# Block 1's mixer in another order: two RWKV chains among the projections, three output tiles open at once

## The chip, the cores and the metric

The kernel runs on one core of a Trainium2 chip. The metric is the device time of one execution in microseconds; a smaller time is better. The profile is of one execution on that core. Its engines are TensorE (PE; PEld is its weight load), VectorE (DVE), ScalarE (ACT), GpSimd (POOL) and SyncE (SP), which issues the transfers. Each engine takes its instructions strictly in the order of its own queue.

## What is computed

The reference runs three model blocks one after another on one sequence of 512 positions with 1024 channels, in float32. The change touches the mixer of the first block only:

```python
h = rmsnorm(x, norm_mix) * (1 + sc1) + sh1          # sc1, sh1, g1 ... from silu(c) @ w_mod + b_mod
p_fox, p_rwkv, p_moba = split(h @ w_in)
y_fox  = fox_attention(fq, fk, fv, ff)              # 4 heads of 64, causal softmax, forget gates added to the logits
y_rwkv = rwkv7_time_mix(p_rwkv, ...)                # 8 heads of 64, recurrence S_t = S diag(w) - (S kk)(kk a)^T + v k^T
y_moba = moba_attention(mq, mk, mv)                 # 4 heads of 64, blocks of 256: over 512 positions plain causal softmax
x = x + g1 * (concat(y_fox, y_rwkv, y_moba) @ w_out)
```

Behind it come the feed-forward part of block 1, a second block (attention, gating and convolution layers) and a third (state-space and convolution mixer).

## The kernel before

Activations lie with channels on the partitions, as tiles of 128 x 512. A float32 product is made of three products of the faster type: weights and activations are each split into a high part and a rest, and `mm3` (L298 to L300) issues high x high, high x rest and rest x high for each slice of 128 input channels. `wsplit` brings a weight tile: SP loads `wr` (two buffers), ACT casts it to `wh` (L277), DVE subtracts to `wl` (L279); `wh` and `wl` have three buffers each. `fm` makes one output tile of 128 channels in 24 matmuls of 512 columns, `tm` (L372 to L374) the two value projections with tokens on the partitions. PSUM has four tags, `mm`, `pa`, `pb` and `pt`, of two buffers each.

The mixer, `block1_mix`, consists of generators that issue work piece by piece:

- `keys` and `proj_rv` make the RWKV projections (keys; receptance and value) of four tiles, two heads each. `proj_rv` forms RO on POOL (L1017), the bonus on DVE (L1018) and sums it over a head on PE (L1023). After the fourth, `proj_r` makes the gate's projection `gl`.
- `proj_fox` and `proj_moba` make the values, then four query and key tiles each (`fqk`, tag `aq`).
- `blocks` (`rwkv_blocks`) prepares for each tile the inverse of a triangular matrix: a product on PE, the 16 x 16 diagonal blocks gathered over DRAM by SP, then 15 rounds of two small operations on DVE (L728, L729, here called the block chain), a cast to VT on ACT (L731, L732), a write to DRAM (L734) and a read back as T and TT (L737).
- `inverses` (`rwkv_inverse`) doubles the blocks to 128 x 128: products on PE (L752 is the first that needs T, L757, L760, and so on), copies on ACT, subtractions on DVE.
- `chain` (`rwkv_chain`) is the recurrence over four pieces of 128 positions, for one tile: transposes (L815), products among keys (L695, masked on DVE, L831, to `Ak`), L843 with `Ak`, then for each piece L853 to L872, which go from PE to ACT (L858) to PE to DVE (L854, L870, L872) and back; last the output (L879 to L882), a group norm (L887 to L896, its power on POOL, L895), a transpose (L900) and the gate (L906, L907).
- the two causal attentions (`attn`): two head pairs, per pair eight steps over 128, 256, 384 and 512 keys, for two heads each. A step's first half is logits on PE (L623, for fox L626, then L627 the mask) in `pt`, the maximum `nmx` on DVE (L565) and `P`, the exponential, on ACT (L568); its second half transposes `P` on PE (L577), copies it to `PT` on ACT (L580), multiplies by the values (L585) and scales on ACT (L590). The second half of a step is issued behind the first half of the next. A finished pair is transposed (L596), copied to `ya` (L618) and split (L286, L289). The four results are `yf0`, `yf1` (fox) and `ym0`, `ym1` (moba).
- `mods` makes the modulation vectors: a weight tile times a row and a sum over it on DVE, in one piece (L395) or in two halves (L386).

The order in which the pieces are issued is written by hand as two strings, one letter for one piece of a generator: `ORDER` (L2105) for the projections, with k keys, r receptance and value, f fox, m moba, b blocks, i inverses, a fox attention; then `REST` (L2103), with 0 to 3 for the four chains, i, a fox, m moba attention, d modulation. What they leave is woven (`weave`). A scheduler then places every instruction in its engine's queue by this priority and by the time at which it takes its inputs to be ready. Behind it, all output tiles are made from eight slices of input: `yf0`, `yf1`, the four chains' results, `ym0`, `ym1`.

In the kernel before the four chains run beside the fox and moba attention. Chains 0 and 1 use `pa` and `pb`, chains 2 and 3 both `mm`; the eight output tiles use `mm` one after another (the last two together).

## Time and profile before

| | us |
|---|---|
| median of 3 timed runs | 3099.59 |
| lowest and highest of them | 3094.19, 3102.67 |
| the profiled execution | 3092.06 |
| its span, first to last instruction | 3090.3 |
| mean granted TensorE clock over it | 0.975 of full |
| PE busy | 2911.2 (94%) |
| DVE busy | 2031.3 (66%) |
| ACT busy | 1164.4 (38%) |
| POOL busy | 679.0 (22%) |

The mixer of block 1 takes the first 512 us or so of the span: projections from some 30 us, the fox attention from 296 us, output tiles from 451 us. In a timeline a line gives start, length, engine, line, operation and tiles; "x4" are four in a row, and brackets tell how long the engine was idle before and what ended it. PEclk is the clock that TensorE was granted, as a share of 2.4 GHz; a 0.5 is 1.2 GHz. The matmuls are pipelined: their listed lengths overlap, and the time between two starts is what one costs.

### The profile page before, as it was taken

The numbers are of one execution on the slowest core, as the hardware profiler recorded it, in microseconds if no ns is written. First come the engines' busy times: TensorE is split into PE (matmuls) and PEld (weight loads), VectorE is DVE, ScalarE is ACT, GpSimd is POOL, SyncE is SP. The second block draws the span as 40 slices with busy tenths as digits, with TensorE's granted clock in tenths as the row PEclk, the third lists the DMA queues.
The fourth block names the chain that finished last, engine by engine and source line by source line (L and its number), as shares of the span: only waits on it lengthen the run. The fifth ranks groups of instructions, "written<-read, shape, count | busy, mean of one in ns | idle before, by whom it ended". The sixth has DMA issues, their size and how long they took to land. (4 is left out here: it accounts for less than half of the span.)

```text
span 3090.3 us, 40017 instructions
## 1 busy us (share of the span) xinstructions
PE 2911.2 (94%) x15254; PEld 2436.7 (79%) x15254; DVE 2031.3 (66%) x3398; ACT 1164.4 (38%) x1945; POOL 679.0 (22%) x582
## 2 busy tenths in 40 slices
PE   5999999999999988999999999999899998999998
PEld 3777878888877777888889788888788877877776
DVE  7766467665458577566564556364786978689764
ACT  4432433323333544332333333233444434442242
POOL 3222011000144253200001120001133333323312
PEclk9998999999999999999999999999999999999999
DMA  6334024463322123236343223333212222333332
GB/s 225 102 108 139 17 94 150 120 211 100 89 76 82 52 86 103 79 102 198 102 149 118 69 89 93 99 97 93 84 55 85 66 82 60 111 109 116 97 112 79
DMA packets 139681, 316.74 MB, mean 102 GB/s; under 512 B 25760, under 2 KB 51936, under 8 KB 139488
## 3 DMA queue, kind: packets, MB, share of 16 engines
q1 hardware_dynamic: 139488, 314.18, 32.9%
q8 instruction: 120, 1.97, 0.3%
q14 instruction: 73, 0.60, 0.1%
HBM read 298.92 MB, written 15.20 MB: 102 GB/s over the span
## 5 line engine op out<-in xcount | busy, mean ns | idle before, releaser
L279 DVE TENSOR_TENSOR wl<-wr,wh 128x1024 fp32r<-128x1024 f32 (+2 forms) x415 | 506.1, 1220 | 474.0 <-ACT wh L277 455.9
L277 ACT CAST wh<-wr 128x1024 fp32r<-128x1024 f32 (+2 forms) x457 | 455.7, 997 | 955.2 <-PE mm L299 461.3
L298 PE MATMUL mm<-hi,wh 128*128 128x512 f32 (+1 forms) x1844 | 711.3, 387 | 9.5 <-ACT csg L1396 4.2
L300 PE MATMUL mm<-hi,wl 128*128 128x512 f32 (+1 forms) x1844 | 708.0, 384 | 10.3 <-DVE wl L279 10.3
L299 PE MATMUL mm<-lo,wh 128*128 128x512 f32 (+1 forms) x1844 | 708.0, 385 | 2.2 <-DVE lo L289 1.2
L298 PEld LDWEIGHTS mm<-hi,wh 128*128 128x128 f32 x1844 | 351.6, 191 | 82.4 <-ACT csg L1396 5.5
L300 PEld LDWEIGHTS mm<-hi,wl 128*128 128x128 f32 x1844 | 352.5, 191 | 80.8 <-DVE wl L279 12.3
L299 PEld LDWEIGHTS mm<-lo,wh 128*128 128x128 f32 x1844 | 351.9, 191 | 71.5 <-DVE lo L289 2.7
L288 POOL CAST hi<-us 128x512 fp32r<-128x512 f32 x66 | 42.4, 643 | 873.6 <-DVE us L1196 855.3
L300 PE MATMUL pt<-hi,wl 128*128 128x512 f32 (+1 forms) x485 | 175.8, 363 | 4.0 <-DVE wl L279 4.0
L298 PE MATMUL pt<-hi,wh 128*128 128x512 f32 (+1 forms) x485 | 175.1, 361 | 0.0
L299 PE MATMUL pt<-lo,wh 128*128 128x512 f32 (+1 forms) x485 | 175.0, 361 | 0.0
L372 PE MATMUL mm<-wh,hi 128*128 128x256 f32 (+1 forms) x512 | 151.0, 295 | 18.8 <-DVE cv L1219 8.8
L298 PE MATMUL pb<-hi,wh 128*128 128x512 f32 (+1 forms) x445 | 165.2, 371 | 0.0
L299 PE MATMUL pb<-lo,wh 128*128 128x512 f32 (+1 forms) x445 | 165.0, 371 | 0.0
L300 PE MATMUL pb<-hi,wl 128*128 128x512 f32 (+1 forms) x445 | 164.9, 371 | 0.0
L300 PE MATMUL pa<-hi,wl 128*128 128x512 f32 (+1 forms) x420 | 161.3, 384 | 0.0
L298 PE MATMUL pa<-hi,wh 128*128 128x512 f32 (+1 forms) x420 | 160.9, 383 | 0.0
L299 PE MATMUL pa<-lo,wh 128*128 128x512 f32 (+1 forms) x420 | 160.8, 383 | 0.0
L1417 DVE SCALAR_TENSOR_TENSOR u<-csg,vec,u 128x400 f32<-128x400 f32 (+9 forms) x208 | 157.7, 768 | 3.7
L373 PE MATMUL mm<-wl,hi 128*128 128x256 f32 (+1 forms) x512 | 148.2, 290 | 0.8 <-DVE wl L279 0.6
L456 POOL TENSOR_TENSOR acc<-acc,sq 128x512 f32<-128x512 f32 (+1 forms) x63 | 86.7, 1385 | 281.2 <-ACT sq L451 230.8
(757 smaller groups left out, 5613.9 us busy)
## 6 DMA issues: line engine op xcount, KB each, us to landing
wr<-f_up SPq DMA_DIRECT2D x88, 512.0 KB, 3.5
wm<-w_mod SPq DMA_DIRECT2D x152, 256.0 KB, 5.0
wr<-w3x SPq DMA_DIRECT2D x56, 512.0 KB, 3.6
wr<-w_up SPq DMA_DIRECT2D x44, 512.0 KB, 3.6
wr<-w3c SPq DMA_DIRECT2D x40, 512.0 KB, 3.6
wr<-f_down SPq DMA_DIRECT2D x32, 512.0 KB, 3.5
wr<-w SPq DMA_DIRECT2D x29, 512.0 KB, 3.6
wr<-w_down SPq DMA_DIRECT2D x16, 512.0 KB, 3.6
```

The lines of the kernel that those rows point to most:

```text
L277: nc.scalar.copy(h, r)
L279: self.lo_engs[self.nlo % len(self.lo_engs)].tensor_tensor(l, r, h.bitcast(FT), OP.subtract)
L288: getattr(nc, hi_eng).tensor_copy(h, x)
L298: nc.tensor.matmul(ps, a, xh, start=first and i == 0, stop=False)
L299: nc.tensor.matmul(ps, a, xl, start=False, stop=False)
L300: nc.tensor.matmul(ps, b, xh, start=False, stop=last and i == n - 1)
L372: nc.tensor.matmul(ps, xh, a, start=k == 0, stop=False)
L373: nc.tensor.matmul(ps, xh, b, start=False, stop=False)
L456: (eng or nc.gpsimd).tensor_tensor(acc[:, hs], acc[:, hs], s, OP.add)
L1417: nc.vector.scalar_tensor_tensor(r8(o)[:, :, a:b], src, w(k), r8(o)[:, :, a:b], OP.mult, OP.add)
```

## The change

The chains get buffer tags of their own. `rwkv_chain` takes three more arguments: the tag of what lives through the chain (the transposed tiles and the state S), the tag of short-lived tiles, and that of the second set of products. Chains 0 and 1 now have PSUM tag `pt` and take their tiles from `aq` (chain 1 also from `g`), where the queries and keys lie; chains 2 and 3 have `pa` and `pb`.

The chains are created before the loop over `ORDER`, and 0 and 1 are issued inside it: chain 0 from behind the third group of inverse pieces, chain 1 behind it. The gate's projection, which a chain's end needs, becomes a generator of its own (g) and comes early. The fox values come later, the queries and keys of both attentions last, those of moba beside the first fox steps. `REST` has chains 2 and 3 beside the fox attention and the moba attention behind it, with the modulation pieces (d) spread. The first six output tiles go to `mm`, `pa`, `mm`, `pb`, `mm`, `pa`, so that three can be open at once, filled with the slices that are ready while the moba attention runs.

```diff
-    def rwkv_chain(self, i, K, gl, out, tag):
+    def rwkv_chain(self, i, K, gl, out, tag, kept, short, short2):
...
-            tok[nme] = self.t2(nm="tok" + nme, tag="h")
+            tok[nme] = self.t2(nm="tok" + nme, tag=kept)
...
-        def inner(lhs, rhs, strict, scale=None, tag="i"):
+        def inner(lhs, rhs, strict, scale=None, tag=short):
...
-        RV = self.t2(nm="RV", tag="i")
+        RV = self.t2(nm="RV", tag=short)
...
-        S = self.t2(nm="S", tag="h")
+        S = self.t2(nm="S", tag=kept)
...
-        A = list(zip(inner(kt, RO, 0), inner(bt, RO, 0, d2, "g")))
+        A = list(zip(inner(kt, RO, 0), inner(bt, RO, 0, d2, short2)))
...
-        wa, gl = self.t2(nm="wa"), self.accs[1]
+        wa, gl = self.t2(nm="wa"), [self.accs[1]]
...
-            yield from self.rwkv_chain(i, P[i], gl, yr[i], tag)
+            yield from self.rwkv_chain(i, P[i], gl[0], yr[i], *tag)
...
-            self.mix_evac(self.fm(A["w1"][1], xs), 1, gl)
-            self.sigmoid(gl, gl)
+
+        def proj_g():
+            self.mix_evac(self.fm(A["w1"][1], xs), 1, gl[0])
+            self.sigmoid(gl[0], gl[0])
             yield
...
-        gens = dict(k=keys(range(4)), f=proj_fox(), m=proj_moba(), r=proj_r(), i=inv, a=None, d=md, b=blocks())
+        ch = [chain(i, CTAG[i]) for i in range(4)]
+        gens = dict(k=keys(range(4)), f=proj_fox(), m=proj_moba(), r=proj_r(), g=proj_g(), i=inv, a=None, d=md, b=blocks())
+        gens.update(zip("0123", ch))
...
-        for c in "kbfmr":
+        for c in "kbfmrg":
...
-        ch = [chain(i, CTAG[i]) for i in range(4)]
...
-            done(i, self.fm(A["w_out"][i], ys))
+            done(i, self.fm(A["w_out"][i], ys, WOT[i]))
...
-CTAG = ("pa", "pb", "mm", "mm")
+CTAG = (("pt", "aq", "aq", "aq"), ("pt", "aq", "g", "g"), ("pa", "h", "i", "g"), ("pb", "h", "i", "g"))
+WOT = ("mm", "pa", "mm", "pb", "mm", "pa")
...
-REST = "aaiiidaiaiaiaiaiaaaaaaaaaaaaaaaaaaaaaaa0aaaa21ammmmdd0m1323mmmdd0123mmmmdd0123mm2mmdd013mmdmimd0121d3m2mmd03mmmmdd0123mdmmmdd012m3mmmdd"
+REST = "2a3a2a3ad2a3aad2aa3aad2aa3aad2aa3aad2aa3aad2aa3aadamamammmmdmmmdmmmdmmmdmmmdmmmd"
...
-ORDER = "krkrbbkfiiirribbkfriiirbfibfmfbiiiibrraiimmmamaiaaaaa"
+ORDER = "krkrbbkiiirribb0k0gr0iii0r0bi0b0r001f1iii1bi1r1b1f1f1f1fiiifmimamamamaaaa"
```

In the new code the lines of the mixer stand one to four further down (L728 is unchanged, L1018 becomes L1019, L1146 becomes L1150). Three places show what the new strings do to the queues; each tile's number tells instances apart.

The first is DVE's queue in the block chain of inverse 0, from its step of 48 elements a row. Before:

```order
L688 RECIPROCAL d_147_739<-d_147_739 128x8
L728 TENSOR_TENSOR btmp_628<-UV_624 64x48
L1045 TENSOR_TENSOR fz_742<-mm_783,fb 128x4
L729 TENSOR_TENSOR UV_624<-UV_624,btmp_628 64x4x12
L728 TENSOR_TENSOR btmp_628<-UV_624 64x55
L729 TENSOR_TENSOR UV_624<-UV_624,btmp_628 64x5x11
L728 TENSOR_TENSOR btmp_628<-UV_624 64x60
L729 TENSOR_TENSOR UV_624<-UV_624,btmp_628 64x6x10
L728 TENSOR_TENSOR btmp_628<-UV_624 64x63
L729 TENSOR_TENSOR UV_624<-UV_624,btmp_628 64x7x9
```

and now:

```order
L728 TENSOR_TENSOR btmp_628<-UV_624 64x48
L279 TENSOR_TENSOR wl_1174<-wr_1172,wh_1173 128x1024
L729 TENSOR_TENSOR UV_624<-UV_624,btmp_628 64x4x12
L635 SCALAR_TENSOR_TENSOR rM_866<-mm_867,vec_94,rM_866 128x511
L728 TENSOR_TENSOR btmp_628<-UV_624 64x55
L1019 SCALAR_TENSOR_TENSOR kp_536<-rM_866,vec_94,kp_536 128x512
L729 TENSOR_TENSOR UV_624<-UV_624,btmp_628 64x5x11
L728 TENSOR_TENSOR btmp_628<-UV_624 64x60
L729 TENSOR_TENSOR UV_624<-UV_624,btmp_628 64x6x10
L728 TENSOR_TENSOR btmp_628<-UV_624 64x63
```

Between the steps L728 and L729 there stood only the sum L1045 for the fox forget gates; now a weight split (L279), the evacuation of a receptance tile (L635) and the bonus (L1019) stand there. The product that waits for the bonus (tile kp_536) is the bones matmul on PE.

The second is DVE's queue at the first steps of the fox attention, with nmx (L565) and the modulation tiles (L395). Before:

```order
L780 TENSOR_SCALAR TT_2072<-pb_2398 64x4x64
L395 SCALAR_TENSOR_TENSOR wm_3202,modr<-wm_3202,act 128x1024
L395 SCALAR_TENSOR_TENSOR wm_3319,modr<-wm_3319,act 128x1024
L1127 TENSOR_TENSOR mod<-modr,vec_94 128x8
L395 SCALAR_TENSOR_TENSOR wm_3397,modr<-wm_3397,act 128x1024
L635 SCALAR_TENSOR_TENSOR acc_87<-mm_2409,vec_94,acc_87 128x511
L565 TENSOR_REDUCE nmx_2448<-pt_2444 128x1
L565 TENSOR_REDUCE nmx_2459<-pt_2455 128x1
L789 TENSOR_TENSOR X_2466<-X_2466,pa_2468 128x512
L570 RECIPROCAL rinv_2453<-sm_2451 128x1
L395 SCALAR_TENSOR_TENSOR wm_3418,modr<-wm_3418,act 128x1024
```

and now:

```order
L565 TENSOR_REDUCE nmx_2777<-pt_2773 128x1
L570 RECIPROCAL rinv_2782<-sm_2780 128x1
L395 SCALAR_TENSOR_TENSOR wm_3030,modr<-wm_3030,act 128x1024
L395 SCALAR_TENSOR_TENSOR wm_3088,modr<-wm_3088,act 128x1024
L395 SCALAR_TENSOR_TENSOR wm_3242,modr<-wm_3242,act 128x1024
L395 SCALAR_TENSOR_TENSOR wm_3299,modr<-wm_3299,act 128x1024
L395 SCALAR_TENSOR_TENSOR wm_3512,modr<-wm_3512,act 128x1024
L565 TENSOR_REDUCE nmx_2862<-pt_2858 128x1
L395 SCALAR_TENSOR_TENSOR wm_3539,modr<-wm_3539,act 128x1024
L570 RECIPROCAL rinv_2867<-sm_2865 128x1
L279 TENSOR_TENSOR wl_3928<-wr_3926,wh_3927 128x1024
L565 TENSOR_REDUCE nmx_2880<-pt_2876 128x1
```

Before, all but one of the twelve L395 stood ahead of the first nmx; now ten of them stand behind it, five in a row between two nmx, and the split of the first output weights (wl_3928) among them.

The third is PE's queue at the end of the second moba pair. Before, with the ends of the chains (L900, L906) and the first output tile (L298, L299):

```order
L623 MATMUL pt_3799<-fqk_2367,fqk_2301 128x512
L627 MATMUL pt_3799<-mnegR,identR 128x128
L577 MATMUL pt_3809<-cst,P_3783 128x128 x4
L900 MATMUL mm_3846<-cst,yt_3736 128x128 x4
L906 MATMUL mm_3855<-acc_87,lora_437 128x512
L900 MATMUL mm_3878<-cst,yt_3767 128x128 x4
L585 MATMUL pt_3816<-fv_1724,PT_3814 128x64
L585 MATMUL pt_3816<-fv_1751,PT_3814 128x64
L585 MATMUL pt_3816<-fv_1778,PT_3814 128x64
L585 MATMUL pt_3816<-fv_1805,PT_3814 128x64
L577 MATMUL pt_3858<-cst,P_3804 128x128 x4
L906 MATMUL mm_3887<-acc_87,lora_437 128x512
```

and now, from the last step but one:

```order
L577 MATMUL pt_3870<-cst,P_3852 128x128 x4
L585 MATMUL pt_3877<-fv_2567,PT_3875 128x64
L585 MATMUL pt_3877<-fv_2594,PT_3875 128x64
L585 MATMUL pt_3877<-fv_2621,PT_3875 128x64
L585 MATMUL pt_3877<-fv_2648,PT_3875 128x64
L596 MATMUL pt_3883<-cst,yt_3748 128x128 x4
L298 MATMUL mm_3925<-hi_3920,wh_3927 128x512
L298 MATMUL pa_3974<-hi_3920,wh_3976 128x512
L298 MATMUL mm_4025<-hi_3920,wh_4027 128x512
L299 MATMUL mm_3925<-lo_3921,wh_3927 128x512
L300 MATMUL mm_3925<-hi_3920,wl_3928 128x512
L299 MATMUL pa_3974<-lo_3921,wh_3976 128x512
```

The chains' ends are gone from here, and so are the output matmuls that stood beside the last step. The three open tiles (mm_3925, pa_3974, mm_4025) take the slice ym1 (hi_3920, lo_3921) together behind the last transpose, L596; the tiles behind them need new weights. Between PE rows 1343 and 1378 of this queue there are only L577, L585, L623 and L627.

## Rows read from the trace of the kernel before

**Rows 1.** The page, part 1: busy time, share of the span, instructions

```profile
PE 2911.2 (94%) x15254; PEld 2436.7 (79%) x15254; DVE 2031.3 (66%) x3398; ACT 1164.4 (38%) x1945; POOL 679.0 (22%) x582
```

**Rows 2.** By stretch: length, busy time of each engine, PEclk, DMA share, GB/s

```profile
96.00:221.00 125.00, 117.39 (x710) 99.75 (x708) 84.59 (x191) 44.73 (x76) 31.92 (x32) 0.95 0.36 100
221.00:258.00 37.00, 33.51 (x159) 27.71 (x156) 23.14 (x60) 8.58 (x15) 12.78 (x10) 0.72 0.35 94
258.00:295.00 37.00, 36.85 (x195) 29.86 (x193) 21.02 (x32) 8.75 (x14) 6.99 (x5) 1.00 0.47 156
295.00:316.00 21.00, 18.15 (x96) 15.08 (x94) 17.09 (x31) 11.04 (x26) 4.68 (x6) 0.76 0.51 170
316.00:440.00 124.00, 122.64 (x883) 98.92 (x882) 60.28 (x177) 47.36 (x142) 8.20 (x11) 0.97 0.14 47
440.00:454.00 14.00, 9.16 (x48) 7.14 (x48) 10.04 (x17) 5.63 (x13) 7.90 (x6) 0.88 0.12 39
454.00:469.00 15.00, 15.00 (x66) 12.19 (x65) 15.00 (x37) 5.95 (x9) 2.22 (x1) 1.00 0.55 177
```

**Rows 3.** Timeline of PE: start, length, line; in brackets the idle before

```profile
96.24 0.39 PE L372 MATMUL mm<-wh,hi 128*128 128x260 f32 x1
...
119.75 0.39 PE L300 MATMUL mm<-hi,wl 128*128 128x512 f32 x1
119.97 0.39 PE L298 MATMUL mm<-hi,wh 128*128 128x512 f32 x1
...
123.38 1.09 PE L752 MATMUL pa<-T,W 128*128 128x128 f32 x4 [2.79 <-DMA T<-ivd]
...
301.37 0.33 PE L577 MATMUL pt<-cst,P 128*128 128x128 f32 x1 [2.37 <-ACT P L568]
```

**Rows 4.** Timeline of DVE, at and behind the block chain

```profile
102.43 1.24 DVE L728 TENSOR_TENSOR btmp<-UV 64x15 f32<-64x15 f32 x1
...
104.39 0.17 DVE L728 TENSOR_TENSOR btmp<-UV 64x28 f32<-64x28 f32 x1
...
112.80 0.17 DVE L729 TENSOR_TENSOR UV<-UV,btmp 64x15 f32<-64x15 f32 x1
...
117.81 1.22 DVE L279 TENSOR_TENSOR wl<-wr,wh 128x1024 fp32r<-128x1024 f32 x1 [1.99 <-ACT wh L277]
118.95 0.74 DVE L635 SCALAR_TENSOR_TENSOR rM<-mm,vec,rM 128x511 f32<-128x511 f32 x1
119.73 1.87 DVE L1018 SCALAR_TENSOR_TENSOR kp<-rM,vec,kp 128x512 f32<-128x512 f32 x1
```

**Rows 5.** Timeline of GpSimd (POOL), at the chain's first step

```profile
102.34 1.30 POOL L677 TENSOR_TENSOR bt<-bt,kt 128x512 f32<-128x512 f32 x1 [3.78 <-ACT kt L672]
```

**Rows 6.** Timeline of ScalarE (ACT), behind the chain's last step

```profile
113.31 0.65 ACT L732 CAST VT<-UV 64x256 fp32r<-64x256 f32 x1
```

**Rows 7.** Groups by line and shape, 295 to 475: busy, mean ns, idle

```profile
L386 DVE SCALAR_TENSOR_TENSOR wm<-wm,act 128x512 f32<-128x512 f32 x24 | 15.9, 681 | 0.0
L565 DVE TENSOR_REDUCE nmx<-pt 128x1 f32<-128x512 f32 x8 | 5.5, 688 | 11.9 <-PE pt L627 11.9
L395 DVE SCALAR_TENSOR_TENSOR wm<-wm,act 128x1024 f32<-128x1024 f32 x4 | 5.0, 1246 | 0.1
...
L277 ACT CAST wh<-wr 128x1024 fp32r<-128x1024 f32 x6 | 6.3, 1054 | 9.6 <-PE mm L299 9.4
L568 ACT ACTIVATION_READ_ACCUMULATOR P<-pt,nmx 128x1 f32 x32 | 6.2, 195 | 0.0
L568 ACT ACTIVATE P<-pt,nmx 128x512 f32<-128x512 f32 x8 | 5.5, 686 | 10.3 <-DVE nmx L565 10.3
L580 ACT COPY PT<-pt 128x512 f32<-128x512 f32 x8 | 4.6, 579 | 0.2
L286 ACT CAST hi<-ya 128x512 fp32r<-128x512 f32 x4 | 2.4, 619 | 0.0
L858 ACT ACTIVATE x<-mm 128x128 f32<-128x128 f32 x8 | 2.2, 281 | 4.1 <-PE mm L857 4.1
```

1 line of the change is left out of this document (added).

## The prediction

> **What bounds the kernel now.** First the page's busy times: TensorE (PE) is busy 94% of the span and no other engine comes near [rows 1], so a change that keeps the work as it is can only take away what PE loses. Next the table by stretches, since the change touches block 1's mixer alone. Up to 96.24 us PE's two orders are the same, row for row: there the kernel before starts the fox value projection [rows 3]. The mixer's last common point is some 469 us, three output tiles done. A stretch loses in two ways: the idle time (length less PE busy) and a clock below full, priced as length times (1 less PEclk), because matmuls take twice as long at the half clock. From [rows 2], stretch by stretch:
>
> 96 to 221: 7.6 idle + 125 x 0.05 = 6.2 of clock; 221 to 258: 3.5 + 10.4; 258 to 295: 0.2 + 0; together 27.9 us while the projections run. 295 to 316: 2.9 + 5.0; 316 to 440: 1.4 + 3.7; 440 to 454: 4.8 + 1.7; 454 to 469: 0; together 19.5 us from the start of the attention to the first output tiles. So 47 us, 1.5% of the span, is the most that any order could win here; it has to be won without new waits. The two losses that the change aims at are the start of the fox attention (the 2.37 us before L577 [rows 3], behind VectorE's (DVE's) mod tiles L395) and the end, 440 to 454, where chains and attention finish together with nothing else to run. In 316 to 440, in contrast, attention and chains hide one another almost wholly: 122.6 of 124 us.
>
> **The change part by part.** The matmuls, casts and loads are the same in number but for merged rows; nothing is removed. What moves is who stands beside whom.
>
> *The block chain of inverse 0.* On DVE the 30 steps L728/L729 run in line, at 0.17 us for the first kind of size [rows 4], and end at 112.97 before. ACT's VT follows to 113.96 [rows 6], two transfers follow that, and PE starts L752 at 123.38 [rows 3]: 9.4 us from VT's end to its use. Behind the same steps DVE now has one wl more (1.22), two L635 (0.74 each), L1018 of the kernel before (0.74 if priced as L635; 1.87 as it ran at 119.73) and two more 512-wide operations (0.74 each), less three L1045 of 0.15: 1.22 + 1.48 + 0.74 + 1.48 - 0.45 = 4.5 us [rows 4]. So the chain ends near 117.5, VT near 118.5, T arrives near 127.9. PE until then has 82 matmuls of 512 columns at the 0.225 us between starts and 33 short ones at about 0.136 (four in 1.09 us at the half clock [rows 3]): 96.2 + 18.5 + 4.5 = 119.2. Two new waits come ahead: the bones product (L1023 of before) needs L1018's output, which DVE reaches around 109.5 while PE is there at 96.2 + 48 x 0.225 + 0.5 = 107.5: 2.0 us. And chain 0's L843 needs Ak, behind the same steps: 0.7. PE then stands at 121.9 and waits 6.0 for T, where it waited 2.79: +3.2. Bounds of this wait: 0 (the two transfers land as soon as PE is there: -2.8) to 8 (L1018 at 1.87 and one step held as below: +5).
>
> DVE steps beside GpSimd are slower: the first L728 took 1.24 us while GpSimd ran its L677 from 102.34 to 103.64, the larger one at 104.39 took 0.17, and L1018 took 1.87 [rows 4, 5]. The Trainium skill, GPSIMD Engine Reference, section 1 (Specifications), says that GpSimd shares its SBUF interfaces with VectorE and contends with instructions that read two SBUF inputs; the steps of the block chain are of that kind and the change puts r's product on GpSimd beside them. By that rule one more step is held for about 1 us, and the sum would be one microsecond higher; by the rows alone it may as well fall between two steps. It is not in the sum.
>
> *Chains 0 and 1 among the projections.* Eight steps, each with a trip from PE to ACT and back (L858, 0.28 us [rows 7]) and one over DVE of the same size. Between the trips stand mostly 4 to 8 matmuls of a projection, 0.9 to 1.8 us. Covered they cost nothing, bare some 0.9 us each: 0 to 7, I take 3.0 with the L843 wait in it, nearer to covered. What is queued behind each such wait on PE is the projection itself, for which everybody waits. The later inverses keep their waits for T; I leave the half clock of 96 to 258 (16.6 us) where it is, since the pauses that precede it stay or grow; bounds -10.4 (the stretch 221 to 258 gone) and +3.4.
>
> Projections: 2.0 + 3.2 + 3.0 = **+8.2** (bounds -13 to +18).
>
> *The attention.* The 19.5 us of 295 to 469 go. Five costs come.
> Mod tiles: twelve L395 of 1.25 us [rows 7] now stand between the first nmx of the fox attention; the five in a row (6.2 us) are hidden by 48 projection matmuls (10.8 us), the later ones stand with one L279 before the next nmx and have no projection beside them: I take the 2.4 us that the same pile cost before L577; 0 to 6.
> Half mod tiles: 24 L386 of 0.68 + 0.08, which stood beside the output tiles (there DVE was busy 15.0 of 15.0 us and PE too, so they cost nothing [rows 2]), stand now between the nmx of the first moba pair, two or three before each: 1.5 to 2.3 us of delay for an nmx, with output matmuls as PE's cover. 0 to 6; 2.0, nearer to the row of 454 to 469.
> The second moba pair is bare: chains, projections and the open output tiles have nothing left for it. After its L627 a step on 512 keys needs nmx 0.69, P 0.69 + 0.20, PT of the step before 0.58 [rows 7], 2.2 us, and PE has four transposes, 0.5: 1.6 us of idleness per step, down to about 0.9 at 128 keys. The first two of eight steps still lie beside the last open matmuls: 6 x 1.25 + 1.5 for the last pair's PT and output = 9.0 (6 to 13).
> The tail: all three open tiles wait for one K slice, ym1: copy 0.58, hi 0.62 with hand-overs, 1.3 us [rows 7]. Behind them the fourth tile's wh needs the slot that the first tile held to the end: ACT's cast of 1.05 starts then, and PE has 4 + 2 matmuls (1.35 us) against two casts and a DVE subtract (1.05 + 1.05 + 1.2): 1.5. Together 2.8 (1.5 to 5).
> The clock: the bare pair is a stretch like 440 to 454; I take that one's 1.7 (0 to 10).
> 2.4 + 2.0 + 9.0 + 2.8 + 1.7 = 17.9, against 19.5: **-1.6** (bounds -12 to +18). What the early chains gain is spent where they are missing.
>
> Sum: 8.2 - 1.6 = **+6.6 us**. The profiled execution took 3092.06 (span 3090.3); with the change 3098.7. It lies 7.5 us below the median of the runs shown, 3099.59, so the median to expect is **3106**. A measurement here can tell some 0.3%, 9.3 us, from no change: the forecast is "no change that can be measured", on the slower side.
>
> **The rivals.**
> *Faster.* The pauses before 258 shrink because chain steps stand between the inverse's steps, PE keeps the full clock in 221 to 258 (-10.4), the wait for T is no longer than before (-3.2 from the sum), the chain steps are covered (-3.0), and the bare pair costs its lower bound (-3), the mod tiles nothing (-4.4): 6.6 - 24 = -17, 3082. For it: the half clock of 221 to 258 is the largest loss, and 258 to 295, full of projections, has none [rows 2]. Against it: the projection matmuls that chains now use as cover are the ones that cover the inverses. Chance 0.30.
> *Slower by the clock of the second moba pair.* The pair is some 24 us of PE work with 9 us of holes. Stretches with such holes ran at 0.76 (295 to 316) and 0.88 (440 to 454), dense ones at 1.00 [rows 2]. At 0.7 over 33 us it costs 10 instead of 1.7, and the pauses between 96 and 221 add a 3.4: 6.6 + 8.3 + 3.4 = +18, 3118. It decides the case as soon as PE is at the half clock for most of the pair. The Trainium skill, TensorE: Matmul & The Clock Gate, Part 1, has the same: the gate grants the clock by how busy PE has been of late; the rows of 295 to 316 and 440 to 454 agree. Chance 0.20.
> *Slower by DVE's queue.* What now stands between the block chain's steps delays every inverse (four of them) by the 4.5 us of the first, with projections used up as cover: two more waits of 5, +17, 3116. It decides where DVE's wait for PE's tiles falls inside the chain. Against it: later chains find fewer projections on DVE. Chance 0.12.
> *It doesn't do what it says.* The new buffer tags are shared with the query and key tiles; if a chain's buffer comes free late, chains 0 and 1 stop PE among the projections and end no earlier than in the attention. The time is then that of before or a little more, 3100 to 3108. Chance 0.04, inside "no change".
>
> **How the numbers follow.** Forecast 0.34 and the last rival 0.04 give no change within 0.3%: 0.38. Faster 0.30; slower 0.20 + 0.12 = 0.32. The bounds of the terms give 3075 to 3136 if half of them fall on one side; the range 3074 to 3134 leaves about one in ten out on each side.
>
> **What would show it.** In the profile after: a wait of about 2 us before the bones product and of 5 to 6 before the first L752; PE idle for about 1.2 us in each of the last six moba steps, behind ACT's PT; 1 to 3 us of idleness around the last K slice; no gap of several us at the chains' ends; PEclk below full around the inverses as now. Wrong would be the term of the projections if the first L752 waits under 3 us, that of the attention if the last moba pair runs without gaps, and the whole if PE's half-clock time before 258 falls under 10 us.

## The result and the profile after

The changed kernel takes 3119.25 us (median of 14 runs, 3111.13 to 3133.64) where the kernel before, run beside it, takes 3100.11 (14 runs). The ratio on record is 1.0054, 95% interval 1.0032 to 1.0076 (the two medians alone give 1.0062). It is slower by 0.54%, more than the 0.3% that can be told from no change. The time lies inside the range on record, on the side that the sum gave, but 13 us above it.

The first lines answer to [rows 1] and to the clock of the table of before: span and mean granted clock, then the busy times of the page.

```profile
core 0: 3128.5 us, clock 0.966
...
PE 2941.3 (94%) x15254; PEld 2456.1 (79%) x15254; DVE 2029.1 (65%) x3398; ACT 1164.6 (37%) x1945; POOL 676.4 (22%) x582
```

The instructions are the same in number, and yet PE is busy 30 us longer than in [rows 1]: matmuls at the half clock take nearly twice as long (in the rows further down, products of 512 columns start every 0.43 us at the half clock and every 0.23 at the full one). Next the stretches, with the columns of [rows 2]; 96 to 338 is projections, 338 to 440 the fox attention with chains 2 and 3, 440 to 472 the first moba pair, 472 to 506 the second.

```profile
96.00:126.00 30.00, 26.59 (x137) 21.17 (x136) 24.26 (x51) 11.74 (x20) 7.14 (x9) 0.97 0.38 101
126.00:152.00 26.00, 25.49 (x104) 21.99 (x103) 9.76 (x15) 5.44 (x9) 8.22 (x7) 0.51 0.15 48
...
258.00:338.00 80.00, 78.56 (x489) 66.57 (x488) 42.98 (x94) 22.88 (x40) 13.87 (x12) 1.00 0.35 103
338.00:350.00 12.00, 8.09 (x38) 6.12 (x37) 6.79 (x12) 3.54 (x8) 0.28 (x1) 0.84 0.84 293
350.00:440.00 90.00, 87.56 (x483) 70.27 (x482) 41.97 (x118) 30.66 (x86) 6.05 (x7) 0.76 0.23 74
440.00:472.00 32.00, 30.61 (x152) 21.76 (x150) 20.42 (x66) 13.18 (x39) 1.46 (x1) 1.00 0.19 58
472.00:506.00 34.00, 26.03 (x80) 17.62 (x81) 6.66 (x14) 11.91 (x28) 0.00 (x0) 0.56 0.00 0
```

Two kinds of loss show. In 338 to 350 and in 472 to 506 PE is idle (3.9 and 8.0 us). In 126 to 152, in part of 350 to 440 and in 472 to 506 it runs at the half clock, in the first two almost without idle time. The places of PE's idle time, in its timeline (columns of [rows 3]):

```profile
122.44 1.10 PE L844 MATMUL pt<-tokv,Ak 128*128 128x64 f32 x8 [1.99 <-DVE Ak L832]
...
126.63 1.09 PE L752 MATMUL pa<-T,W 128*128 128x128 f32 x4
...
346.31 0.69 PE L585 MATMUL pt<-fv,PT 128*128 128x64 f32 x2 [3.91 <-ACT PT L580]
...
469.97 0.40 PE L299 MATMUL mm<-lo,wh 128*128 128x512 f32 x1
470.20 0.40 PE L300 MATMUL mm<-hi,wl 128*128 128x512 f32 x1
...
473.04 0.66 PE L585 MATMUL pt<-fv,PT 128*128 128x64 f32 x4 [1.13 <-ACT PT L580]
...
476.41 1.11 PE L585 MATMUL pt<-fv,PT 128*128 128x64 f32 x4 [1.37 <-ACT PT L580]
...
481.23 1.54 PE L585 MATMUL pt<-fv,PT 128*128 128x64 f32 x6 [1.06 <-ACT PT L580]
...
487.14 1.54 PE L585 MATMUL pt<-fv,PT 128*128 128x64 f32 x6 [1.30 <-ACT PT L580]
...
493.16 1.97 PE L585 MATMUL pt<-fv,PT 128*128 128x64 f32 x8 [1.20 <-ACT PT L580]
...
496.66 1.97 PE L585 MATMUL pt<-fv,PT 128*128 128x64 f32 x8 [0.68 <-ACT PT L580]
...
500.83 0.80 PE L298 MATMUL mm<-hi,wh 128*128 128x512 f32 x1 [1.32 <-ACT hi L286]
...
502.28 0.63 PE L299 MATMUL mm<-lo,wh 128*128 128x512 f32 x1
502.71 0.63 PE L300 MATMUL mm<-hi,wl 128*128 128x512 f32 x1
```

The reader is to see that the first L752 has no bracket any more (2.79 in [rows 3]), that its place is taken by chain 0's L844, and that the six holes of the last pair follow one another: the rows left out between them are the pair's own L577, L596, L623 and L627.

**Two sums instead of one.** The same program's runs spread by 20 to 45 us, which hides differences of ten. Each run lists its span and its mean granted clock, and these split the time: span times clock is what it would have taken at full clock, span times (1 less clock) what the half clock took. The table has the mean over the runs of each kernel and its standard error. Runs more than 1.5% above the fastest of the same kernel are left out, here and in the ratios (two each of e7_one and e11_wide, one each of e1_fill, e10_tail and e16a_one0): 3154.84 us of e11_wide, a little above its limit, would raise the 85.8 to 89.4.

| kernel | runs | median us | ratio to before, interval | at full clock | taken by half clock |
|---|---|---|---|---|---|
| before | 58 | 3097.1 | | 3014.0 ± 0.3 | 84.8 ± 1.7 |
| after (with e0_again) | 25 | 3122.7 | 1.0054 [1.0032, 1.0076]; again 1.0073 [1.0043, 1.0103] | 3023.2 ± 0.5 | 97.0 ± 2.0 |
| e1_fill | 5 | 3127.5 | 1.0108 [1.0065, 1.0152] | 3034.5 ± 1.1 | 93.9 ± 4.1 |
| e11_wide | 10 | 3115.2 | 1.0045 [1.0009, 1.0081] | 3031.6 ± 1.2 | 85.8 ± 4.6 |
| e7_one | 4 | 3143.3 | 1.0133 [1.0087, 1.0179] | 3016.5 ± 1.4 | 121.6 ± 5.8 |
| e10_tail | 11 | 3120.6 | 1.0046 [1.0012, 1.0080] | 3021.0 ± 0.8 | 93.8 ± 4.2 |
| e5_none | 6 | 3135.2 | 1.0109 [1.0066, 1.0153] | 3014.1 ± 1.2 | 122.4 ± 5.4 |
| e6_wot | 12 | 3106.7 | 1.0017 [0.9987, 1.0047] | 3014.2 ± 0.7 | 91.7 ± 3.4 |
| e3_mods | 6 | 3147.0 | 1.0155 [1.0119, 1.0191] | 3024.4 ± 1.5 | 120.6 ± 2.6 |
| e14_nomod | 7 | 3117.5 | 1.0104 [1.0067, 1.0141] | 3020.3 ± 0.7 | 102.7 ± 5.4 |
| e16a_one0 | 5 | 3133.3 | 1.0108 [1.0063, 1.0153] | 3018.5 ± 1.5 | 109.6 ± 9.1 |
| e16b_one0 | 6 | 3147.4 | 1.0161 [1.0129, 1.0192] | 3017.3 ± 1.7 | 127.4 ± 4.9 |

Over these runs the change costs 9.2 us at full clock and 12.2 (± 2.7) of half clock. The two sums are not quite independent: over the 58 runs of the kernel before, the first falls by 0.16 us (± 0.015) for each us that the second rises. Idle time at the half clock counts half in each, and 0.43 us is less than twice 0.23. If the same slope holds between kernels, the first sum hides some 6 us of what e5_none costs, which has 38 us more half clock than the kernel before, and 2 us of what the change costs.

From the traces comes the split by stage, from 96 us to the first mask product L627 of the fox attention, and from there to the same row of the feed-forward part: the sum of PE's idle times of 0.4 us and more, the time at the half clock (it costs matmuls a little under half of that), and PE's work in both stages (length less idle time; of what is left, half-clock time counted half).

| profile | idle, projections | half clock there | idle, rest of the mixer | half clock there | work |
|---|---|---|---|---|---|
| before | 11.0 | 34.1 | 9.5 | 27.3 | 508.7 |
| before, again (e17_before) | 11.9 | 54.6 | 10.2 | 27.3 | 507.4 |
| after | 10.6 | 37.5 | 16.4 | 85.3 | 510.5 |
| after, again (e0_again) | 11.0 | 47.8 | 18.6 | 37.5 | 513.9 |
| e5_none | 18.2 | 98.3 | 7.7 | 24.5 | 508.3 |
| e7_one | 18.9 | 96.9 | 10.3 | 47.8 | 508.1 |
| e10_tail | 11.5 | 23.9 | 15.2 | 34.1 | 513.7 |
| e11_wide | 11.8 | 37.5 | 15.8 | 13.7 | 519.5 |
| e14_nomod | 11.5 | 37.5 | 14.6 | 37.5 | 512.4 |
| e16b_one0 | 11.1 | 99.0 | 9.2 | 75.1 | 508.5 |

The projections keep their idle time; the attention's rises by 7 to 8 us. PE's work rises by 2 to 6 in the table. Part of that is that 96 us is not the same row in every profile: from the row at which the two queues part (96.24 us in before, 95.82, 96.03 and 97.90 in the three others) it rises by 2 to 4, 3 in the mean. The matmuls are the same, so they start further apart; where, I have not traced. Idle time within a half-clock stretch counts half as full clock and half as half clock in the first table. Some 7 of the last pair's 8 us lie so; with that, 7.5 of idle time and 3 of work less 3.3 give some 7 of the 9.2, and of the 12.2 some 9 are the matmuls' own. The other 2 us are no more than the rest of the span differs between the two profiles of one kernel.

### The profile page after: what moved, and what is told of

Same layout as the page of the kernel before. It is cut to its first block, busy times and chain, and to the rows that moved or that the text cites. A ratio compares the mean times of both kernels' runs of the same rounds, so it can differ in the third digit from the quotient of the medians.

```text
span 3128.5 us, 40021 instructions
## 1 busy us (share of the span) xinstructions
PE 2941.3 (94%) x15254; PEld 2456.1 (79%) x15254; DVE 2029.1 (65%) x3398; ACT 1164.6 (37%) x1945; POOL 676.4 (22%) x582
## 3 DMA queue, kind: packets, MB, share of 16 engines
q8 instruction: 120, 1.97, 0.3%
## 5 line engine op out<-in xcount | busy, mean ns | idle before, releaser
L279 DVE TENSOR_TENSOR wl<-wr,wh 128x1024 fp32r<-128x1024 f32 (+2 forms) x415 | 505.6, 1219 | 472.3 <-ACT wh L277 458.1
L298 PE MATMUL mm<-hi,wh 128*128 128x512 f32 (+1 forms) x1820 | 703.5, 387 | 11.1 <-ACT csg L1400 4.4
L300 PE MATMUL mm<-hi,wl 128*128 128x512 f32 (+1 forms) x1820 | 698.1, 384 | 10.3 <-DVE wl L279 10.3
L299 PE MATMUL mm<-lo,wh 128*128 128x512 f32 (+1 forms) x1820 | 699.1, 385 | 2.7 <-DVE lo L289 1.6
L298 PEld LDWEIGHTS mm<-hi,wh 128*128 128x128 f32 x1820 | 346.6, 191 | 83.7 <-ACT csg L1400 5.6
L299 PEld LDWEIGHTS mm<-lo,wh 128*128 128x128 f32 x1820 | 346.9, 191 | 71.1 <-DVE lo L289 3.6
L298 PE MATMUL pt<-hi,wh 128*128 128x512 f32 (+1 forms) x485 | 175.2, 361 | 0.0
L299 PE MATMUL pt<-lo,wh 128*128 128x512 f32 (+1 forms) x485 | 175.1, 361 | 0.0
L298 PE MATMUL pb<-hi,wh 128*128 128x512 f32 (+1 forms) x453 | 169.2, 373 | 0.0
L299 PE MATMUL pb<-lo,wh 128*128 128x512 f32 (+1 forms) x453 | 168.8, 373 | 0.0
L298 PE MATMUL pa<-hi,wh 128*128 128x512 f32 (+1 forms) x436 | 167.4, 384 | 0.0
L299 PE MATMUL pa<-lo,wh 128*128 128x512 f32 (+1 forms) x436 | 167.2, 383 | 0.0
```

Of the source, the lines that this page charges most:

```text
L279: self.lo_engs[self.nlo % len(self.lo_engs)].tensor_tensor(l, r, h.bitcast(FT), OP.subtract)
L298: nc.tensor.matmul(ps, a, xh, start=first and i == 0, stop=False)
L299: nc.tensor.matmul(ps, a, xl, start=False, stop=False)
L300: nc.tensor.matmul(ps, b, xh, start=False, stop=last and i == n - 1)
```

## The experiments

Three theories are tried. The pair theory: the loss is the bare second moba pair, by its holes and by the half clock in it. The projections theory: it is the projections, by chain steps there and by the query and key projections moved last, which take the inverses' cover (work that PE has to do while it would otherwise wait). The tiles theory: it is the twelve L395 at the fox attention's start.

**e0_again** is the changed kernel once more.

> The changed kernel once more, for a second profile and times beside the other runs. Theory (the attention starves at its end, and the half clock comes on top): again PE idle 1.0 to 1.4 us in each of the last six moba steps and about 1.3 us before the last K slice, and the wait of some 4 us before L585 at the first fox steps. The 41 us at the half clock from 394 to 435 us has no pause in front of it; the changed kernel's times fall into two groups, near 3112 and near 3126, some 17 us apart, and half of 41 is 20: if that stretch makes the groups, a profile with a time near 3112 lacks it and one near 3126 has it. Rival (the projections are what made it slower): the stretches up to 340 us differ as much between two profiles as the times do.

Its ratio is 1.0073 [1.0043, 1.0103]. PE's idle times repeat to a few hundredths of a microsecond in the last pair (1.13, 1.36, 1.06, 1.30, 1.20, 0.68; before L298 1.32). The half-clock stretches don't repeat: the same part of the fox attention with chains 2 and 3, first in after, then in e0_again (columns of [rows 2]):

```profile
394.00:435.00 41.00, 40.64 (x173) 33.94 (x170) 16.09 (x50) 8.55 (x24) 2.55 (x2) 0.50 0.27 85
```

```profile
399.50:422.50 23.00, 21.98 (x173) 18.31 (x169) 15.35 (x49) 8.30 (x24) 1.65 (x1) 1.00 0.38 122
```

The same rows take 41 us in the first and 23 in the second. PE was dense ahead of both (9.47 and 9.46 us busy of the 10 before) and still the clock fell in one. So this stretch of after isn't the change's. Nor does it make the two groups of times: the profiled run of e0_again took 3123.57 us and lacks it. Only what stands in several profiles, or in the means over the runs, may be charged to it. The 30.7 us at the half clock in the last pair do repeat, in all four profiles that have this pair unchanged (after, e0_again, e3_mods, e14_nomod).

**e1_fill** and **e11_wide** put matmuls that nobody reads into the holes: ahead of the transposes in the last six steps of the second moba pair, 16 of 128 columns or 4 of 512.

```diff
-            psP = self.pst(tag2)[:, :nk]
+            psP = self.pst(tag2)
+            for j in range(fill if pr == 1 and 2 * qt + hh > 1 else 0):
+                nc.tensor.matmul(psP[:, j % 4 * 128:j % 4 * 128 + 128], self.identR, self.mnegR, start=True, stop=True)
+            psP = psP[:, :nk]
...
-        moba = self.causal_attn(*P["moba"], P["mobav"], ym)
+        moba = self.causal_attn(*P["moba"], P["mobav"], ym, fill=16)
```

```diff
-            psP = self.pst(tag2)[:, :nk]
+            psP = self.pst(tag2)
+            for j in range(fill if pr == 1 and 2 * qt + hh > 1 else 0):
+                nc.tensor.matmul(self.V4(psP), self.identR, self.B4(self.mnegR), start=True, stop=True)
+            psP = psP[:, :nk]
...
-        moba = self.causal_attn(*P["moba"], P["mobav"], ym)
+        moba = self.causal_attn(*P["moba"], P["mobav"], ym, fill=4)
```

> The changed kernel with sixteen 128-column matmuls of constants put ahead of the transposes of P in the last six steps of the second moba pair; nobody reads them, everything else keeps its place in every queue. They are some 0.9 us of PE work per step, where PE idles 1.2. Theory (the holes bring the half clock, and it costs more than they do): the granted clock stays full from 470 to 500 us or comes back sooner, and the stretch from the first bare step to the first following output tile shortens from 40 us by 8 to 12 us although 5.4 us of matmuls were added; median lower by as much. Rival 1 (the holes alone cost, the clock falls anyway): the half clock stays 25 us or more in this stretch, time equal or up to 5 us more. Rival 2 (PE's work counts here, not the latency): 5 us or more slower.

> As the run with sixteen matmuls of 128 columns in each of the last six steps of the second moba pair, but with four of 512 columns: the same 0.9 us of PE work in the same places. There the clock fell all the same (44 us at the half clock from 448 us) and the pair took longer. Theory A (not the holes but the kind of work sets the clock there: short matmuls, many waits): with four long ones the stretch from 460 to 505 us keeps the full clock or gets it back within some 10 us, the half clock takes 85 to 92 over the runs, the time at the full clock 3025 to 3030. Theory B (any idle stretch of this pattern brings it): 25 us or more at the half clock there, and no gain over the changed kernel.

The pair in e1_fill, then in e11_wide (columns of [rows 2]; PEclk is the third number from the end):

```profile
448.00:493.00 45.00, 40.51 (x151) 32.59 (x151) 6.02 (x12) 11.07 (x24) 0.00 (x0) 0.51 0.00 1
```

```profile
445.00:479.00 34.00, 28.06 (x141) 19.26 (x142) 6.45 (x18) 13.82 (x39) 0.00 (x0) 0.99 0.00 1
```

With the short ones the clock stood at half all the same (44.4 us) and the fillers, at half clock, only made the pair longer. With the wide ones it stayed at full through the pair, and over the runs the half clock took 85.8 instead of 97.0: 11 us (± 5) less. Some 3 of them are the idle time that no longer lies at the half clock, the other 8 what the clock costs the pair's matmuls; by the trace of after it is half of 30.7 less 7, 12 us. My sum had 1.7. The 11 are little more than two standard errors, and each filler has one profile; what in the wide fillers holds the clock isn't shown. At full clock e11_wide takes 8.4 us more (24 fillers at 0.22 are 5.3 of it), so that little is left of the gain. The pair theory is borne out: holes and half clock of this pair repeat, and the half clock goes with the wide fillers.

**e5_none** takes chains 0 and 1 back beside the attentions, with the `REST` of before, and keeps the rest of the new order: receptance and gate early, fox values later, all query and key projections last. **e7_one** takes chain 1 alone back, beside the moba attention.

```diff
-CTAG = (("pt", "aq", "aq", "aq"), ("pt", "aq", "g", "g"), ("pa", "h", "i", "g"), ("pb", "h", "i", "g"))
+CTAG = (("pa", "h", "i", "g"), ("pb", "h", "i", "g"), ("mm", "h", "i", "g"), ("mm", "h", "i", "g"))
...
-ORDER = "krkrbbkiiirribb0k0gr0iii0r0bi0b0r001f1iii1bi1r1b1f1f1f1fiiifmimamamamaaaa"
+ORDER = "krkrbbkiiirribbkgriiirbibrfiiibirbffffiiifmimamamamaaaa"
```

```diff
-CTAG = (("pt", "aq", "aq", "aq"), ("pt", "aq", "g", "g"), ("pa", "h", "i", "g"), ("pb", "h", "i", "g"))
+CTAG = (("pt", "aq", "aq", "aq"), ("mm", "h", "i", "g"), ("pa", "h", "i", "g"), ("pb", "h", "i", "g"))
...
-REST = "2a3a2a3ad2a3aad2aa3aad2aa3aad2aa3aad2aa3aad2aa3aad2aa3aadamamammmmdmmmdmmmdmmmdmmmdmmmd"
+REST = "2a3a2a3ad2a3aad2aa3aad2aa3aad2aa3aad2aa3aad2aa3aad1amam1ammmm1mdmm1mdm1mmdm1mmd1mmmd1mmmd"
...
-ORDER = "krkrbbkiiirribb0k0gr0iii0r0bi0b0r001f1iii1bi1r1b1f1f1f1fiiifmimamamamaaaa"
+ORDER = "krkrbbkiiirribb0k0gr0iii0r0bi0b0r00fiiibirbffffiiifmimamamamaaaa"
```

> The main part undone alone: chains 0 and 1 are taken out of the projections and all four chains run beside the attentions with the second string, PSUM tags and tile tags of the kernel before; the projections keep the new sequence (gate early, queries and keys of both attentions last) and the output tiles the three open buffers. Theory (the chains are what covers the waits for T now that the queries and keys come last): waits of 3 to 6 us before the first L752 of inverses 1 to 3, with stretches of 20 to 30 us at the half clock behind them, as in the run with one chain; the half clock takes 110 or more; median 3125 to 3150, slower than the changed kernel although the second moba pair has no holes. Rival (the chains among the projections are the loss): median at or under 3100, the kernel before.

> Half of the change undone: only chain 0 stays among the projections, chain 1 goes back beside the moba attention in PSUM tag mm with the tile tags of the kernel before; the three open output tiles stay. By the order of the queue chain 1 now fills the first moba pair and the output matmuls come into the second: all but two of its steps have matmuls beside them. Theory (the attention starves because its cover was spent early): the holes of 1.0 to 1.4 us in the second pair go, with them most of the half clock from 476 to 506 us, and the projections get shorter by the part of chain 1; 12 to 25 us faster than the changed kernel, so at or below the kernel before. Rival (the projections' new waits, first of all that of inverse 0, are the loss): these stay, since chain 0 stays; gain under 6 us.

In e5_none the holes of the last pair are gone, and at full clock it is level with the kernel before, 3014.1 (some 6 us more when its half clock is allowed for; its projections have 18.2 us of idle time instead of 11 to 12). But the half clock takes 122 us, and the timeline shows why, the first L752 of the four inverses:

```profile
128.20 1.09 PE L752 MATMUL pa<-T,W 128*128 128x128 f32 x4 [4.58 <-DMA T<-ivd]
...
194.42 0.87 PE L752 MATMUL pa<-T,W 128*128 128x128 f32 x3 [3.52 <-DMA T<-ivd]
...
249.61 0.66 PE L752 MATMUL pa<-T,W 128*128 128x128 f32 x2 [3.34 <-DMA T<-ivd]
...
300.17 0.44 PE L752 MATMUL pa<-T,W 128*128 128x128 f32 x1 [3.36 <-DMA T<-ivd]
```

The half clock begins during each wait or at its end and lasts 30.7, 27.3, 27.3 and 27.3 us. One of them by its window:

```profile
249.00:277.00 28.00, 27.39 (x120) 24.58 (x121) 11.83 (x22) 3.62 (x7) 7.32 (x6) 0.51 0.15 51
```

PE is busy for 27.39 of these 28 us, at 1.2 GHz. e7_one shows the same at the inverses whose chain 1 went away (waits of 4.97 and 3.46 us, then 30.7 and 27.3 us at half) and not at the first, which chain 0 still covers; a third stretch of 27.3 us, at the second inverse, stands behind a wait of 1.29 us only. Expected 12 to 25 us faster than the changed kernel, e7_one is slower, 1.0133.

So the change has two sides. The new order of the projections costs some 38 us of half clock by itself. That this comes from the queries and keys, which no longer cover the inverses, and not from the other moves in the same string, is argued from the waits and not tested. The chains put in their place give about 25 of that back, and cost 9 us at full clock (some 5 when the difference in half clock is allowed for), because the attentions have lost them. The projections theory holds for the new order, the pair theory for the chains.

**e10_tail** leaves chain 1 among the projections but holds its last three pieces for the moba attention, in PSUM tag `mm`.

```diff
-ORDER = "krkrbbkiiirribb0k0gr0iii0r0bi0b0r001f1iii1bi1r1b1f1f1f1fiiifmimamamamaaaa"
+ORDER = "krkrbbkiiirribb0k0gr0iii0r0bi0b0r001f1iii1bi1r1bffffiiifmimamamamaaaa"
...
-REST = "2a3a2a3ad2a3aad2aa3aad2aa3aad2aa3aad2aa3aad2aa3aad2aa3aadamamammmmdmmmdmmmdmmmdmmmdmmmd"
+REST = "2a3a2a3ad2a3aad2aa3aad2aa3aad2aa3aad2aa3aad2aa3aad1amam1ammmm1mdmm1mdmmmdmmmdmmmdmmmd"
```

> The changed kernel with the last three pieces of chain 1 (its second products, its output and its end) taken out of the projections and put beside the first moba pair, in PSUM tag mm; its first five pieces stay among the projections, where they stand before the T waits of inverses 1 to 3. Two measures per run: the time at the full clock (span times granted clock; 3023 over 25 runs of the changed kernel, 3014 over 16 of the kernel before, each to 2.5) and what the half clock takes (span times one less the clock; 97 and 86). Theory (chain 1 is needed as cover in both places: with it all back beside the attention the waits for T of 5.0 and 3.5 us came up and 27 to 31 us of half clock behind each): waits for T stay under 1.3 us as in the changed kernel, three or four of the six holes in the second moba pair are filled, time at the full clock 3014 to 3019, the half clock takes 85 to 100, median 3100 to 3117. Rival (any chain work taken from the projections lets the half clock in there): the half clock takes 110 or more, median above 3125.

It gains 2.2 us at full clock and 3 (± 5) of half clock: the first moba pair's output tiles move up, but 1.38, 1.20 and 0.68 us of holes stay in the second, with 13.7 us at half clock instead of 30.7. At 1.0046 it can't be told from the changed kernel, and 3021.0 at full clock misses the 3014 to 3019 expected.

**e6_wot** is the kernel before with only the three open output tiles.

```diff
+WOT = ("mm", "pa", "mm", "pb", "mm", "pa")
...
-            done(i, self.fm(A["w_out"][i], ys))
+            done(i, self.fm(A["w_out"][i], ys, WOT[i]))
```

> The kernel before with the three open output tiles alone (tags mm, pa, mm, pb, mm, pa). By the queue's order only the second tile can start some slices early, for chains 2 and 3 end last and the tiles wait for them. Theory (open tiles do nothing without early chains): time at the full clock 3011 to 3016, the half clock's share unchanged (80 to 92), median within 0.3% of the kernel before. Rival (they cover the waits at the chains' ends, 4.8 us idle from 440 to 454): 4 to 8 us faster at the full clock.

3014.2 at full clock against 3014.0: this part changes nothing while chains stand beside the attention.

**e3_mods** spreads the twelve L395 and their loads among the projections (the letters d go from `REST` into `ORDER`); **e14_nomod** leaves them out, so that the modulation vectors lack them and only its time means anything.

```diff
-ORDER = "krkrbbkiiirribb0k0gr0iii0r0bi0b0r001f1iii1bi1r1b1f1f1f1fiiifmimamamamaaaa"
+ORDER = "krkrbbkiiirribb0k0gr0diii0r0bdi0b0rd00d1f1iiid1bid1rd1bd1f1df1fd1fdiiifdmimamamamaaaa"
```

```diff
+        nc.vector.memset(raw, 0.0)
...
-                mod_some(1)
```

> The changed kernel with the twelve L395 modulation tiles and their loads issued one by one among the projections instead of in a row at the first fox steps. Theory (the wait of 3.9 us before L585 at 346 us comes from nmx queued behind L395 on DVE, which waits for w_mod's loads; with it go 6.8 us of half clock, 3.4): that wait is gone, the start of the fox attention is 5 to 7 us shorter, the rest the same, if the loads find room among the projections. Rival (the loads only collide elsewhere): DVE waits for w_mod or ACT for wr among the projections, and the 96 to 340 us stretch grows by as much; time the same within 4 us.

> The changed kernel without the twelve L395 modulation tiles that the sequence places before the fox attention's start, and without their loads (the first part of the shift, scale and gate columns is then zero: left out of the computation, so only the time means anything). Theory 'the 3.9 us wait before L585 at the fox attention's start, and half-clock time behind it, are these tiles' price': the wait at that L585 goes to under 0.7 us, time at full clock falls by 3 to 5 us (3018 to 3020 instead of 3023), time taken by the half clock falls by 2 to 4 (93 to 95). Theory 'the half-clock stretches around the fox attention belong to the attention with chains 2 and 3 itself': full clock time falls alike, but the time taken by the half clock stays at 97 within 3. If the total falls by less than 2 us, the pile of tiles costs nothing and something else (the quadrant memory of nmx) makes that wait.

How the twelve stop the fox attention in after is read from DVE's and SP's timelines:

```profile
335.31 1.22 DVE L395 SCALAR_TENSOR_TENSOR wm<-wm,act 128x1024 f32<-128x1024 f32 x1
335.43 7.84 SPq L390 DMA_DIRECT2D wm<-w_mod  x6
...
339.39 1.23 DVE L395 SCALAR_TENSOR_TENSOR wm<-wm,act 128x1024 f32<-128x1024 f32 x1 [2.85 <-DMA wm<-w_mod]
...
341.68 1.22 DVE L395 SCALAR_TENSOR_TENSOR wm<-wm,act 128x1024 f32<-128x1024 f32 x1 [1.06 <-DMA wm<-w_mod]
...
343.87 1.23 DVE L395 SCALAR_TENSOR_TENSOR wm<-wm,act 128x1024 f32<-128x1024 f32 x1 [0.96 <-DMA wm<-w_mod]
...
345.02 0.42 DVE L565 TENSOR_REDUCE nmx<-pt 128x1 f32<-128x256 f32 x1
```

DVE is not busy, it waits: three L395 in line wait 4.9 us for their weight tiles (512 KB each, a median of 6.0 us from issue to landing there), and nmx, which needs none of them, stands behind them. Without the twelve the 3.91 us before L585 are gone (nothing over 0.4 there) and 2.9 us at full clock with them; the half clock doesn't follow (102.7 ± 5.4 against 97.0), so its 6.8 us behind that wait can't be shown to be the tiles' price. For the same reason the total doesn't fall (1.0104). The expectation took that as the sign of another cause, but the trace decides: with the tiles the wait is gone. Spread among the projections they cost more than here: waits for T of 2.44 and 2.77 us, each with 27.3 us at half clock behind it, and 24 us in the mean. The tiles theory is right in place and small in size.

**e16a_one0** and **e16b_one0** look for a version that keeps both covers: the order of before, chain 0 alone among the projections. They differ in where its steps and the fox projections stand, and in chain 0's tile tags (`g` in the first, `aq` and `g` in the second). The edits are shown against the kernel before; `CTAG` and `REST` change to match.

```diff
-ORDER = "krkrbbkfiiirribbkfriiirbfibfmfbiiiibrraiimmmamaiaaaaa"
+ORDER = "krkrbbkfiiirribbkf0rgiii0rr0bf0i0bf0mf0b0iiiibraiimmmamaiaaaaa"
```

```diff
-ORDER = "krkrbbkfiiirribbkfriiirbfibfmfbiiiibrraiimmmamaiaaaaa"
+ORDER = "krkrbbkiiirribb0kfr0giii0rr0b0f0i0b0f0mf0bfiiiibraiimmmamaiaaaaa"
```

> The sequence of the kernel before with chain 0 alone moved in among the projections (chain 1 stays beside the attentions, the query and key projections stay where they were) and the three open output tiles. Theory 'what the change loses at full clock comes from the bare second moba pair and from chain steps that take the inverses' cover, and the half clock follows pauses before the inverses': with one chain moved and the cover left in place, full clock time is 3012 to 3018 and half clock costs 80 to 92 us; total 3092 to 3106, the kernel before within 0.3%. Theory 'any chain step among the projections costs its 4 to 5 us at full clock': full 3018 to 3022, total 3105 to 3115.

> As the one before, but chain 0 starts one projection step earlier and the fox query and key projections are spread out behind its steps, so that more projection work is left for the later inverses. Theory 'the waits before the inverses decide the half clock': waits for T under 1.3 us, half clock takes 75 to 88 us, full 3012 to 3018, total 3088 to 3104. If the waits are short and the half clock still takes over 95 us, that theory is wrong.

Both are slower than the kernel before, by 1.1% and 1.6%: 4.5 and 3.3 us at full clock, the rest half clock. The 109.6 and 127.4 us of half clock lie above what either was expected to take, and the full-clock times, 3018.5 ± 1.5 and 3017.3 ± 1.7, lie where the two theories of e16a_one0 meet: they don't decide whether a chain among the projections has a price of its own. e16b_one0 speaks against a simple form of the projections theory, though its waits for T were not the short ones wanted. It waits no longer in the projections than before (11.1 us in all, one wait of 3.50), and yet has 99 us of half clock there; and beside the attention the clock fell to half with no wait of 0.8 us or more in the 70 us ahead of it, and stayed there while PE was never idle:

```profile
427.00:437.00 10.00, 9.57 (x60) 6.49 (x61) 5.77 (x18) 3.09 (x10) 0.00 (x0) 1.00 0.09 27
437.00:495.00 58.00, 58.00 (x236) 48.61 (x237) 21.11 (x69) 12.31 (x35) 2.17 (x1) 0.50 0.21 68
```

What makes the clock fall there stays open.

**e17_before** is the kernel before once more.

> The kernel before once more, unchanged, for a second profile of it. Theory 'the instructions' order fixes PE's pauses, and only the length of the half-clock stretches behind them changes from execution to execution': PE's pauses over 1 us in block 1 stand at the same instructions with the same length within 0.2 us (1.99 to 2.8 us before the first L752 and 2.4 us before L577 at the fox attention's start), the half-clock time of block 1's mixer is another than in the first profile by 5 us or more, and span times granted clock is again 3014 within 4. Theory 'the half-clock stretches belong to places of the program': the same stretches within 4 us each, one of 17 to 24 us behind the third inverse among them.

```profile
123.93 0.63 PE L752 MATMUL pa<-T,W 128*128 128x128 f32 x4 [2.21 <-DMA T<-ivd]
...
178.78 0.63 PE L752 MATMUL pa<-T,W 128*128 128x128 f32 x4 [2.19 <-DMA T<-ivd]
...
311.02 0.33 PE L577 MATMUL pt<-cst,P 128*128 128x128 f32 x1 [2.21 <-ACT P L568]
```

The waits stand at the same instructions, those before the L752 half a microsecond longer or shorter (2.21 for the 2.79 of [rows 3], 2.19 for 1.67), the others within 0.2; two of 0.49 and 0.81 us are new. The half-clock time of the mixer is 81.9 us against 61.4; the 20.5 us behind the third inverse are there again, a 23.9 behind the second is new. So the stretches have preferred places, and which of them a run gets differs. Span times clock is 3016.

## Why the prediction came out as it did

The sum was +6.6 us. Without its clock terms it was +15.3: 8.2 of waits in the projections and 7.1 in the attention (16.2 of new idle time against 9.1 that goes, 2.9 + 1.4 + 4.8 of [rows 2]). Its clock terms were -8.7 (10.4 that go, 1.7 that come). Measured were 7.5 of idle time, some 3 of work that the sum did not have, and about 9 of clock. The right direction thus came from two errors of opposite sign.

- **The bones product, 2.0: wrong.** DVE was late as said: L1019 ran at 107.21, held to 1.87 us, one step behind it to 1.29 and a later one to 1.20, these two beside GpSimd's L749 (from 108.89 and 110.64). So the held step that the prediction left out of its sum came twice. But PE came later too, at 109.61, and did not wait. My PE time left out the 1.37 us before L685, a wait that the trace of before has as well (1.47).
- **The wait of 5 to 6 for T, +3.2: wrong.** The block chain ended at 118.6 and VT at 119.6 (117.5 and 118.5 in the sum, about right), and T's first read, issued at 122.6, took 3.9 us. It arrived at 126.5; PE came at 126.63, not at 121.9. It had lost 1.4 at L685 and 1.99 at L844 (0.7 in the sum), some 1.2 by the half clock from 124.3 on, and had 52 short matmuls instead of 33. The time on record as the mark of a wrong step, a first L752 that waits under 3 us, is what the trace shows. The wait was not saved, it was filled by the chain's steps: without them (e5_none) it is 4.58.
- **Chain steps, 3.0:** beside 1.37 at L685 stand 1.99 at L844, 1.81 at chain 0's end (L901) and nine waits of 0.4 to 0.8 us, five of them at chain steps. They took the place of waits for T; the projections' idle sum is 10.6 to 11.0 against 11.0 to 11.9. A step that failed is "the projection matmuls that chains use as cover are the ones that cover the inverses": the chains' own matmuls are cover as well.
- **The half clock of the projections, left where it is:** right on the mean of the profiles (37.5 and 47.8 us against 34.1 and 54.6), for a reason I didn't have: two large shifts, of e5_none's kind and back, that cancel.
- **The mod tiles, 2.4 (0 to 6):** 3.9 in the profiles, 2.9 by e14_nomod. Place right, mechanism wrong: not DVE's 1.25 each but the wait for their loads, which were issued six at a time only at 335.43.
- **The half mod tiles, 2.0:** waits of 0.48 and 0.43 us at the end of that pair; the rest is hidden by output matmuls.
- **The bare moba pair, 9.0, and the tail, 2.8:** 6.74 us in six holes of 0.68 to 1.37 (1.25 each in the sum) and 1.32 before the last slice. The "first two steps and last pair" that made up 1.5, and the wait for the fourth tile's weight, are not there. Together 8.1 for 11.8. The gaps of several microseconds at the chains' ends, 440 to 454, are gone but for one of 0.7 to 2.1 (L901).
- **The clock of the bare pair, 1.7 (0 to 10): the step that failed by most.** I took it from 440 to 454, at PEclk 0.88. The pair is 34 us at 0.56: 15 by the way [rows 2] is priced (which counts the idle time in it once more), 12 for its matmuls by the trace, 8 by the means of e11_wide. This is the rival "slower by the clock of the second moba pair", which put it at 10 us, with a chance of 0.20; it was the case that came, and the row that I had set aside for it, 295 to 316 at 0.76, was nearer than the one taken. The Trainium skill, TensorE: Matmul & The Clock Gate, Part 1, lets the clock follow how busy PE has been; the bare pair agrees (26.03 of 34 us busy, 0.56), while 58 us at half clock without any idle time in e16b_one0 are not explained by it.

DVE's queue as a rival didn't come: later inverses wait at most 1.1 us for T. That the change doesn't do what it says didn't either.

## What to carry to other kernels

Work that hides waits is worth as much where it is taken from as where it is put: price both ends, first as idle time of PE, then by the clock that PE gets in a stretch left with holes, which here cost about as much (8 to 12 us) as the holes themselves (8). Split every run into span times granted clock and span times the rest; the first repeats to 1 to 2 us over a handful of runs and shows a few microseconds of a change where the second is alike; the second needs ten runs and more. Look at what a queued instruction waits for and not only at how long it takes: three tiles waiting for their loads held the attention's maximum, not the 1.25 us that each took.

## What the runs showed of the hardware

Stretches at 1.2 GHz differ from execution to execution where PE has the same instructions and nearly the same waits: behind the same 1.97 to 1.99 us wait at L844 there were 27.3, 30.7, 3.4, 3.4, 3.4 and 3.4 us in six profiles (after, e0_again, e1_fill, e10_tail, e11_wide, e14_nomod). Before the first L752 of an inverse, all seven waits of 3.3 us or more in e5_none, e7_one and e16b_one0 stood at the head of 27 to 31 us at half clock; waits of 1 to 3 us there had anything from none to 27.3 behind them. The length of a wait doesn't decide by itself: behind 3.2 to 3.9 us before an L585 at the fox attention's start (after, e0_again, e7_one, e10_tail) stood 3.4 to 6.8 us. The half clock also came with no such wait (41.0 us in after, 58.0 in e16b_one0). In runs of the kernel before, it takes 68 to 122 us of the span, which is nearly all of their spread.
